# An encoder layer's feed-forward: three of the second half's seven operands are split into high and low parts when they are formed, and the low parts travel through DRAM

## The chip, the cores and the metric

The kernel runs on one core of a Trainium2 chip. The core has a matrix engine (TensorE, PE in the profile; its weight loads stand apart as PEld), a vector engine (VectorE, DVE), a scalar engine (ScalarE, ACT), a general engine (GpSimd, POOL) and an engine that here only issues transfers (SyncE, SP). All transfers that matter go through one queue of SP, which 16 DMA engines serve. Each engine carries out its own instructions in the order in which they were written down for it, and waits where an instruction needs a result of another engine or a landed transfer. The metric is the device time of one execution in microseconds, less being better. The kernel of before took 2279.1 us (median of 3 runs, 2277.12 to 2284.74).

## The reference

The layer works on 2048 tokens of width 1024 in float32. A normalised and modulated input goes through windowed attention and a two-way mLSTM; their outputs are projected and added to the residual stream `x`. The part in question is what follows, a gated feed-forward of width 2816:

```python
hff = rms_norm(x, g_norm2) * (1.0 + scale2) + shift2
gte, up = jnp.split(hff @ w_ffn_in, 2, axis=-1)
ff = (jax.nn.silu(gte) * up) @ w_ffn_out
return x + gate2 * ff
```

A last `rms_norm` follows. The tolerance asks for more than one pass of the fast float32 matmul (the type `fp32r`) gives, so a product of two float32 operands is made of three matmuls: high times high, high times low, low times high. For this every operand exists as a high part (the value rounded to `fp32r` by a copy) and a low part (value minus high part).

## The kernel before

**The products.** The gate and up projections are worked as a two by two block product with seven block products instead of eight. One side are seven weight operands of a 128-column group (`A11`, `A12`, `S2`, `S1`, `S3`, `S4`, `A22`), the other side seven operands made of the normalised tokens, in this order: `B11`, `B21`, `T2`, `T1`, `T3`, `B22`, `T4`. Some of these are sums or differences of others. A token operand has 512 rows of the contraction and 512 token columns, and lies in SBUF as four tiles of 128x1024: two for its high part, two for its low part.

**The units.** `pair` works one unit: the seven products of one column group with one half of the tokens. Each product has four groups of three matmuls (`mm3`, L56 to L58), so a unit has 84 matmuls of 512 columns. There are 22 units for the first half of the tokens (numbered 0 to 21 here) and 22 for the second (22 to 43). Even units belong to the first block column (`half` 0), odd ones to the second up to the turn; odd units leave more sums to POOL and five result tiles to be stored instead of two. Products 0, 2, 4 and 6 add up in one PSUM bank (`ps1`), products 3 and 5 in another (`ps5`), product 1 has a third (`ps2`). Between two products into the same bank ACT has to read the bank out: `s1` after product 0 (L1615), `u2` after product 2 (L1621), `u3` after product 4 (L1629) from `ps1`, and `c5` after product 3 (L1626) from `ps5`. PE can begin product 2, 4, 6 or 5 only when that reading is done; the product in between is the time that ACT has for it. The six tiles that a unit uses for such results (`s1`, `g0`, `t0`, `u2`, `c5`, `u3`) rotate in a pool of six. The results of a unit are stored to `a_d` in DRAM by the next unit's first statement (`stores()`, L1592), and a tile whose store has not landed can't be written again.

**Beside the products.** After product `u` of a unit `beside(u)` runs: it forms the seven weight operands of the next unit (`weights`, a high part by ACT at L1457 and a low part by DVE at L1458 for each, some sums by POOL first), loads the raw weights for the unit after that (`load_raw`), and from unit 2 on, after products 1, 3 and 5, advances by one step a generator (`norm2`) that prepares the second half's token operands: it normalises two blocks of 512 tokens, turns them with PE transposes (`turned`, banks "b" and "d"), forms the seven operands by sums on DVE and stores them unsplit to `hop_d` in DRAM. The first block is copied only; the second block's part walks through four row groups `k`.

**The turn.** Unit 21 is the last of the first half. The token operands of the second half have to come into the same SBUF tiles, so `refill_ops` loads operand `u` after product `u` of unit 21 (`start`, L1414, two transfers of 512 KB into the low part's tiles), and `finish` splits it: ACT copies it into the high part's tiles (L1418), DVE subtracts in place (L1419). `finish` of operands 0 to 3 runs in unit 21 after products 2, 3, 4 and 6, of operands 4 to 6 in unit 22 after products 0, 1 and 3. No weights are formed in unit 21, since units 21 and 22 use the same ones; the raw weights for unit 23 are loaded after product 6 of unit 21.

```python
if turn:
    if u in (2, 3, 4, 6):
        finish_op(min(u - 2, 3))
    if u == 6:
        raw = load_raw(wseq.popleft())
    return
```

The order on each engine is the order of the statements in this part of the program. SP's order is the order of the `dma_start` calls; its queue has eight completion semaphores, which its transfers take in turn (DMAHW0 to DMAHW7 in the listings), so a transfer is issued only when the one eight places ahead of it has landed.

Of the kernel before, what the change touches and what calls it, by code (L numbers as in the profile page):

```python
# [11 lines left out]
F32 = mybir.dt.float32  # L12
F32R = mybir.dt.float32r
BF16 = mybir.dt.bfloat16
I32 = mybir.dt.int32
AF = mybir.ActivationFunctionType
ALU = mybir.AluOpType
MUL, ADD, SUB, MAX, MIN = ALU.mult, ALU.add, ALU.subtract, ALU.max, ALU.min
# [3 lines left out]
P = 128  # L22
# [14 lines left out]
def hybrid_layer_kernel(  # L37
# [5 lines left out]
    pe, dve, act, pool, sp = nc.tensor, nc.vector, nc.scalar, nc.gpsimd, nc.sync  # L43
# [5 lines left out]
    dp = ctx.enter_context(tc.tile_pool(name="dram", bufs=1, space=DRAM))  # L49
    pp = ctx.enter_context(tc.tile_pool(name="psum", bufs=2, space=PSUM))  # L50

    def bank(tag, name):
        return pp.tile([P, 512], F32, tag=tag, name=name, bufs={"g": 2, "a": 2, "b": 1, "c": 2, "d": 1}[tag])
# [16 lines left out]
    bc_d = dp.tile([HM, NT, 4, P], F32, name="bc_d")  # L70
    gate_d = dp.tile([2, D], F32, name="gate_d")
    hop_d = dp.tile([2, 7, 4, P, 512], F32, name="hop_d")
    wo_d = dp.tile([7, 4, P, 512], F32, name="wo_d")
    a_d = dp.tile([7, DFF // P // 2, P, 2, 512], F32, name="a_d")

# [16 lines left out]
    def rsqrt(pl, v, n, d, tag, bufs=2):  # L92

        vv, hh, yi, a = (pl.tile([P, n], dt, tag=tag + i, name=tag + i, bufs=bufs)
                         for i, dt in (("v", F32), ("h", F32), ("y", I32), ("a", F32)))
        y = yi.bitcast(F32)
        o = 0
        for v_, w, d_ in v if isinstance(v, list) else [(v, n, d)]:
            dve.tensor_scalar(vv[:, o:o + w], v_, 1.0 / d_, EPS, MUL, ADD)
            o += w  # L100
        dve.tensor_scalar(yi, vv.bitcast(I32), -0.5, 1597463007.0, MUL, ADD)
        dve.tensor_scalar(hh, vv, -0.5, None, MUL)
        for _ in range(3):
            dve.tensor_tensor(a, y, y, MUL)
            dve.tensor_tensor(a, a, hh, MUL)
            dve.scalar_tensor_tensor(y, a, 1.5, y, ADD, MUL)
        return y
# [40 lines left out]
    def big(i, name, shape=(P, 2, 512), dt=F32R):  # L148

        return hp.tile(list(shape), dt, tag=f"big{i}", name=name)  # L150
# [28 lines left out]
    def turned(t, xt, k, tag, gs, shift):  # L179

        ps = bank(tag, "trn")
        for i in range(4):
            pe.transpose(ps[:, i * P:(i + 1) * P], xt[i][:, k * P:(k + 1) * P], ident)
        act.activation(t, ps, AF.Identity, bias=shift[:, k:k + 1], scale=gs[:, k:k + 1])
# [794 lines left out]
    for i in range(2 * 96 + 60):  # L979
# [3 lines left out]
        if i == 150:  # L983
            t = s2.tile([P, 512], F32, tag="og", name="mqk", bufs=1)
# [300 lines left out]
    class Rows:  # L1285
# [15 lines left out]
        def new(self):  # L1301
            return xd.tile([P, 512], F32, tag="n2", name="n2", bufs=9)
# [58 lines left out]
    def norm2(hh, z, tags, lead):  # L1361
        n = BO[2 * hh + z]
        xt = [pools["ff"].tile([P, D], F32, tag="xt", name="x1t", bufs=4) for _ in range(4)]
        for i in range(4):
            sp.dma_start(xt[i], x1_d[(4 * n + i) * P:(4 * n + i + 1) * P, :])
        op = {o: hop_d[hh, i] for i, o in enumerate(OPS)}
        new = lambda: xp.tile([P, 512], F32, tag="n2", name="n2", bufs=5)
        for _ in range(lead):
            yield True
        ssq = xp.tile([P, 4], F32, tag="ssq", name="ssq")  # L1370
        for i in range(4):
            jk = xp.tile([P, D], BF16, tag="junk", name="junk", bufs=1)
            act.activation(jk, xt[i], AF.Square, accum_out=ssq[:, i:i + 1])
            yield True
        r = rsqrt(xp, ssq, 4, D, "rs")
        yield True
        yield True
        for i in range(4):
            act.activation(xt[i], xt[i], AF.Copy, scale=r[:, i:i + 1])
            yield True  # L1380
        if z == 0:
            for k in range(KT):
                t = new()
                turned(t, xt, k, tags[k % 2], gs2, mod[:, 3, :])
                yield True
                sp.dma_start(op["B11" if k < 4 else "B21"][k % 4], t)
        else:
            for k in range(4):
                b11, b21, b12, b22, t3 = (new() for _ in range(5))
                sp.dma_start(b11, op["B11"][k])  # L1390
                sp.dma_start(b21, op["B21"][k])
                turned(b12, xt, k, tags[0], gs2, mod[:, 3, :])
                yield True
                turned(b22, xt, k + 4, tags[1], gs2, mod[:, 3, :])
                yield True
                dve.tensor_tensor(t3, b22, b12, SUB)
                dve.tensor_tensor(b12, b12, b11, SUB)
                dve.tensor_tensor(b11, b22, b12, SUB)
                yield True
                dve.tensor_tensor(b21, b21, b11, SUB)  # L1400
                for o, t in (("B22", b22), ("T3", t3), ("T1", b12), ("T2", b11)):
                    sp.dma_start(op[o][k], t)
                yield True
                sp.dma_start(op["T4"][k], b21)

    def refill_ops(hh):


        hls = []

        def start(u):
            hls.append([[big(4 * u + 2 * z + i, OPS[u]) for i in range(2)] for z in range(2)])
            for i in range(2):
                sp.dma_start(hls[u][1][i].bitcast(F32), hop_d[hh, u, 2 * i:2 * i + 2].rearrange("k p t -> p k t"))  # L1414

        def finish(u):
            for hi, lo in zip(*hls[u]):
                act.activation(hi, lo.bitcast(F32), AF.Copy)  # L1418
                dve.tensor_tensor(lo, lo.bitcast(F32), hi.bitcast(F32), SUB)  # L1419

        return hls, finish, start
# [10 lines left out]
    def load_raw(j):  # L1432

        v = lambda t: t.rearrange("p (k c) -> p k c", c=P)
        g = wp.tile([P, D], F32, tag="wraw", name="graw", bufs=1)
        a21 = wp.tile([P, 512], F32, tag="oth", name="A21", bufs=1)
        cg, cu = (slice(o + j * P, o + (j + 1) * P) for o in (0, DFF))
        sp.dma_start(v(g), w_ffn_in[:, cg].rearrange("(k p) c -> p k c", p=P))
        sp.dma_start(v(a21), w_ffn_in[0:512, cu].rearrange("(k p) c -> p k c", p=P))
        return (g, a21) if "ff" not in pools and j else (g, a21, load_a22(j))  # L1440
# [45 lines left out]
    for p in range(NPR):  # L1486
# [15 lines left out]
        for i in range(28):  # L1502
# [15 lines left out]
            if p == 0:  # L1518
# [3 lines left out]
                if i in (17, 21):  # L1522
                    hi, lo = (t[i // 21] for t in wo[6])
# [55 lines left out]
    with tc.tile_pool(name="ff", bufs=1, side="right", reuse_waits="tile") as ff:  # L1579
# [84 lines left out]
        pools["ff"] = ff  # L1664
        pools["xp"] = xp
        norms = deque([norm2(1, 0, "bd", 4), norm2(1, 1, "bd", 1)])
        JO = [m * KH + j for j in range(KH) for m in range(2)]
        units = [(0, j) for j in JO] + [(1, j) for j in reversed(JO)]
        wseq = deque(JO[2:] + JO[-2::-1])
        raw, more_w = (*raws[0], load_a22(KH)), None  # L1670
        for n, (hh, j) in enumerate(units[:-1]):
            ws_, turn = nxt_w, n == NJ - 1
            start = lambda u: None
            if turn:
                hop1, finish_op, start = refill_ops(1)
                assert not norms
            STEPS = (0, 0, 1, 1, 2, 2, 1)

            def beside(u):

                nonlocal nxt_w, raw, more_w
                if n in (0, NJ) and u in (0, 1, 3):
                    finish_op(4 + (u + 1) // 2)
                if turn:
                    if u in (2, 3, 4, 6):
                        finish_op(min(u - 2, 3))
                    if u == 6:
                        raw = load_raw(wseq.popleft())
                    return
                if u == 1:  # L1690
                    more_w = weights(raw)
                for _ in range(STEPS[u]):
                    nxt_w = next(more_w)
                if wseq and u == 6 and n != NJ - 2:
                    raw = load_raw(wseq.popleft())
                if n > 1 and u in (1, 3, 5) and norms and next(norms[0], None) is None:
                    norms.popleft()

            pair(hh, j, ws_, hop, start, beside)
            if turn:  # L1700
                hop = hop1
# [263 lines left out]
```

## Time and profile before

| what | value |
|---|---|
| median of 3 runs | 2279.1 us (2277.12 to 2284.74) |
| the profiled execution | 2279.69 us, span 2277.8 us |
| granted TensorE clock over the span | 0.995 |
| PE, DVE, ACT, POOL busy | 98%, 71%, 47%, 47% |
| first half of the feed-forward's products, units 0 to 21 | 994.6 to 1423.1 us of the span |
| second half, units 22 to 43 | 1423.1 to 1848.6 us |
| most units | 19.04 us from start to start |
| unit 22, the first after the turn | 25.65 us |

The times of the trace count from the span's start. A unit's start is the start of its first matmul in the timeline. Units with a PE transpose beside them are 0.5 us longer for each group of four transposes. Since PE is busy almost all the time, time is lost where PE waits, and the waits of other engines matter only where they end in one of PE's.

### The profile page before, as it was taken

How to read it: one execution, taken by the hardware profiler on the slowest of the kernel's cores; microseconds unless marked ns; L12 is line 12 of the kernel's file. 1: busy time of each engine (PE TensorE's matmuls, PEld its weight loads, DVE VectorE, ACT ScalarE, POOL GpSimd, SP SyncE). 2: the span in 40 equal slices, each digit the busy share in tenths (PEclk: the TensorE clock that was granted, in tenths of full speed). 3: DMA queues.
4: the chain of work that ended last, by engine and by line, in shares of the span. 5: the costliest groups of instructions: out<-in, count | busy, mean ns of one | idle time of the engine just before them, and what ended most of it. 6: DMA issues, size and time to landing. Idle time of an engine off the chain costs nothing.

```text
span 2277.8 us, 32434 instructions
## 1 busy us (share of the span) xinstructions
PE 2224.1 (98%) x10822; PEld 1857.4 (82%) x10822; DVE 1613.4 (71%) x2931; ACT 1059.8 (47%) x2206; POOL 1070.8 (47%) x927
## 2 busy tenths in 40 slices
PE   7999999999999989999999999999999999999998
PEld 4997888888888878788888888788888888888886
DVE  6787677656688887786666776766667665785694
ACT  4533656544677756354445444433333333233452
POOL 1006535334344344436666665656566664692020
PEclk8999999999999999999999999999999999999999
DMA  8577755685766576764343454433333374542452
GB/s 318 174 242 224 229 169 166 185 240 172 206 187 180 173 248 203 261 234 151 109 147 111 154 180 158 161 98 111 97 112 97 111 253 145 167 153 93 146 214 93
DMA packets 352811, 391.28 MB, mean 172 GB/s; under 512 B 21260, under 2 KB 251004, under 8 KB 352644
## 3 DMA queue, kind: packets, MB, share of 16 engines
q1 hardware_dynamic: 352420, 389.18, 52.2%
q8 instruction: 85, 1.39, 0.2%
q14 instruction: 82, 0.67, 0.1%
q10 hardware_dynamic: 224, 0.04, 0.0%
HBM read 269.95 MB, written 119.19 MB: 171 GB/s over the span
## 4 chain that ended last, share of the span: by engine, by line
PE 52%; DVE 3%; issue 1%; DMA 1%; ACT 0%; POOL 0%; SPq 0%; DVEq 0%; ACTq 0%; POOLq 0%
PE fp L57 12%; PE fp L56 12%; PE fp L58 12%; PE fo L58 5%; PE fo L57 5%; PE fo L56 5%; DVE al L1719 1%; PE ops L56 1%; DMA al<-a_d 1%; DVE ra L1862 1%; PE ops L58 1%; PE ops L57 1%; DVE w L1728 0%; DVE T L1419 0%; DMA A<-in_w_ffn_in_dram 0%
## 5 line engine op out<-in xcount | busy, mean ns | idle before, releaser
L498 PE MATMUL gps<-hT,whi 128*128 128x512 f32 x1088 | 395.3, 418 | 0.3 <-DVE cacc L513 0.3
L58 PE MATMUL fo<-w,al 128*128 128x512 f32 x616 | 240.0, 390 | 0.8 <-DVE al L1719 0.8
L57 PE MATMUL fo<-w,ah 128*128 128x512 f32 x616 | 239.7, 389 | 0.0
L56 PE MATMUL fo<-w,ah 128*128 128x512 f32 x616 | 239.7, 389 | 0.0
L498 PE MATMUL gps<-hT,wlo 128*128 128x512 f32 x544 | 226.1, 416 | 0.0
L498 PEld LDWEIGHTS gps<-hT,whi 128*128 128x128 f32 x1088 | 199.3, 189 | 24.5 <-DVE cacc L513 0.7
L56 PE MATMUL fp<-T,S 128*128 128x512 f32 x528 | 206.7, 391 | 1.1 <-ACT s L1615 1.1
L57 PE MATMUL fp<-T,S 128*128 128x512 f32 x528 | 205.8, 390 | 0.0
L58 PE MATMUL fp<-T,S 128*128 128x512 f32 x528 | 205.4, 389 | 0.0
L1719 DVE TENSOR_TENSOR al<-al,ah 128x1024 fp32r<-128x1024 f32 x77 | 117.1, 1525 | 108.2 <-ACT ah L1718 108.1
L1718 ACT ACTIVATE ah<-al 128x1024 fp32r<-128x1024 f32 x77 | 81.6, 1059 | 180.9 <-DMA al<-a_d 173.6
L1458 DVE TENSOR_TENSOR S<-sf,S 128x512 fp32r<-128x512 f32 x86 | 130.4, 1554 | 35.9 <-ACT S L1457 35.6
L1458 DVE TENSOR_TENSOR A<-graw,A 128x512 fp32r<-128x512 f32 x86 | 129.6, 1524 | 15.5 <-ACT A L1457 15.5
L1623 DVE SCALAR_TENSOR_TENSOR g<-t,g 128x512 f32<-128x512 f32 x44 | 43.7, 993 | 133.0 <-ACT t L1622 133.0
L58 PE MATMUL fp<-B,A 128*128 128x512 f32 x352 | 136.9, 389 | 0.0
L56 PE MATMUL fp<-B,A 128*128 128x512 f32 x352 | 136.9, 389 | 0.0
L57 PE MATMUL fp<-B,A 128*128 128x512 f32 x352 | 136.9, 389 | 0.0
L58 PEld LDWEIGHTS fo<-w,al 128*128 128x128 f32 x616 | 115.6, 188 | 25.7 <-DVE al L1719 1.7
L56 PEld LDWEIGHTS fo<-w,ah 128*128 128x128 f32 x616 | 115.6, 188 | 24.1
L57 PEld LDWEIGHTS fo<-w,ah 128*128 128x128 f32 x616 | 115.6, 188 | 24.0
L1462 POOL TENSOR_TENSOR sf<-A,A22r 128x512 f32<-128x512 f32 x43 | 60.9, 1417 | 150.2 <-DMA A22r<-in_w_ffn_in_dram 117.6
L798 POOL TENSOR_SCALAR ap<-ap,adn 128x384 f32<-128x384 f32 (+1 forms) x128 | 71.1, 575 | 122.6 <-PE atp L805 66.0
(418 smaller groups left out, 6174.6 us busy)
## 6 DMA issues: line engine op xcount, KB each, us to landing
al<-a_d SPq DMA_DIRECT2D x77, 512.0 KB, 3.7
wmod<-in_w_mod_dram SPq DMA_DIRECT2D x48, 512.0 KB, 7.1
graw<-in_w_ffn_in_dram SPq DMA_DIRECT2D x43, 512.0 KB, 3.6
a_d<-ka SPq DMA_DIRECT2D x66, 256.0 KB, 4.7
bc<-bc_d SPq DMA_DIRECT2D x64, 256.0 KB, 3.7
hop_d<-n SPq DMA_DIRECT2D x56, 256.0 KB, 4.6
a_d<-u SPq DMA_DIRECT2D x55, 256.0 KB, 4.6
mqk<-qk_d SPq DMA_DIRECT2D x44, 256.0 KB, 3.8
```

What stands on the lines that cost most here:

```text
L56: pe.matmul(o, lh, rh, start=first, stop=False, skip_group_check=skip)
L57: pe.matmul(o, lh, rl, start=False, stop=False, skip_group_check=skip)
L58: pe.matmul(o, ll, rh, start=False, stop=last, skip_group_check=skip)
L498: pe.matmul(ps, w[i == 2][:, k, :], hT[n](i == 1, k), start=(k == 0 and i == 0), stop=(k == KT - 1 and i == 2))
L798: pool.tensor_scalar(self.p[g][:, :self.NK], self.p[g][:, :self.NK], dn[:, g:g + 1], 0.0, MUL, ADD)
L1458: dve.tensor_tensor(t[:, 1, :], f, t[:, 0, :].bitcast(F32), SUB)
L1462: pool.tensor_tensor(f1, a21, a22, ADD)
L1623: dve.scalar_tensor_tensor(g0, t0, 1.0, g0, ADD, MUL)
L1718: act.activation(ah, al.bitcast(F32), AF.Copy)
L1719: dve.tensor_tensor(al, al.bitcast(F32), ah.bitcast(F32), SUB)
L1862: dve.tensor_tensor(ra[i], ra[i], xr, ADD)
```

## The change

Operands 4, 5 and 6 of the second half (`T3`, `B22`, `T4`) are split in the generator `norm2`, not at the turn.

- In the generator, each row group `k` of the second block takes five steps instead of four. In the fourth step ACT copies `t3` and `b22` (128x512 each) as rounded high parts into PSUM banks "b" and "d" (`high`). In the fifth step DVE subtracts these from the tiles in place (`low`, one operand in PSUM), the low parts are stored to a new DRAM tensor `hopl_d`, and ACT copies `b21`, which by then holds `T4`, into bank "d". Its subtraction and store are done at the start of the next row group's first step, or after the last one. The unsplit operands are stored to `hop_d` as before; a low part overwrites its tile once that store has landed.
- At the turn, `start` of operands 4 to 6 loads the unsplit operand into the high part's tiles and the low part into the low part's, four transfers of 512 KB instead of two. `finish` of these operands rounds the high part in place on ACT; DVE's six subtractions of 128x1024 are gone.
- The raw weights at the turn are loaded after product 5 of unit 21 instead of after product 6.

```diff
         else:
+            def high(tag, t):
+                h = bank(tag, "hi").bitcast(F32R)
+                act.activation(h, t, AF.Copy)
+                return h
+
+            def low(t, h, o):
+                dve.tensor_tensor(t.bitcast(F32R), t, h.bitcast(F32), SUB)
+                sp.dma_start(o, t)
+
+            left = None
             for k in range(4):
+                if left:
+                    low(*left)
                 b11, b21, b12, b22, t3 = (new() for _ in range(5))
                 sp.dma_start(b11, op["B11"][k])
                 sp.dma_start(b21, op["B21"][k])
...
                 yield True
+                h3, h22 = high(tags[0], t3), high(tags[1], b22)
                 dve.tensor_tensor(b21, b21, b11, SUB)
                 for o, t in (("B22", b22), ("T3", t3), ("T1", b12), ("T2", b11)):
                     sp.dma_start(op[o][k], t)
                 yield True
+                low(t3, h3, hopl_d[0, k])
+                low(b22, h22, hopl_d[1, k])
+                left = b21, high(tags[1], b21), hopl_d[2, k]
                 sp.dma_start(op["T4"][k], b21)
+                yield True
+            low(*left)
...
             for i in range(2):
-                sp.dma_start(hls[u][1][i].bitcast(F32), hop_d[hh, u, 2 * i:2 * i + 2].rearrange("k p t -> p k t"))
+                ks = slice(2 * i, 2 * i + 2)
+                for z, o in ((0, hop_d[hh, u]), (1, hopl_d[u - 4])) if hh and u > 3 else ((1, hop_d[hh, u]),):
+                    sp.dma_start(hls[u][z][i].bitcast(F32), o[ks].rearrange("k p t -> p k t"))
 
         def finish(u):
+            if hh and u > 3:
+                for hi in hls[u][0]:
+                    act.activation(hi, hi.bitcast(F32), AF.Copy)
+                return
...
-                    if u == 6:
+                    if u == 5:
                         raw = load_raw(wseq.popleft())
```

What this does to the order of instructions is shown at three places. In the listings a row has the line, the operation, the tile written and the tiles read, and the semaphores that it waits for. Line numbers after L1385 are those of each kernel: L1414 of before is L1435 of the changed kernel (the turn's loads), L1438 is L1463 (`graw`, raw weights), L1592 is L1617 (stores of results), L1418 is L1443 or, for rounding in place, L1440, and L1457 is L1482.

SP's queue at the turn before, from operand 4 (`T3`) to the first stores of unit 22:

```order
L1414 DMA T3_15404<-hop_d_74 128x2x512 [waits DMAHW1_49,PE_49]
L1414 DMA T3_15405<-hop_d_74 128x2x512 [waits DMAHW2_49,PE_49]
L1414 DMA B22_15428<-hop_d_74 128x2x512 [waits DMAHW3_49,PE_49]
L1414 DMA B22_15429<-hop_d_74 128x2x512 [waits DMAHW4_49,PE_49]
L1414 DMA T4_15449<-hop_d_74 128x2x512 [waits DMAHW5_49,PE_49]
L1414 DMA T4_15450<-hop_d_74 128x2x512 [waits DMAHW6_49,PE_49]
L1438 DMA graw_15459<-in_w_ffn_in_dram 128x8x128 [waits DMAHW7_49,Activation_49]
L1439 DMA A21_15460<-in_w_ffn_in_dram 128x4x128 [waits DMAHW0_49]
L1445 DMA A22r_15463<-in_w_ffn_in_dram 128x4x128 [waits DMAHW1_49]
L1592 DMA a_d_76<-u3_15300 128x512 [waits DMAHW2_49,DVE_49]
L1592 DMA a_d_76<-c5_15299 128x512 [waits DMAHW3_49,Pool_49]
```

and in the changed kernel, from operand 5 (`B22`) on; four transfers for `T3` stand ahead of these:

```order
L1435 DMA B22_15477<-hop_d_74 128x2x512 [waits DMAHW1_49,PE_49]
L1435 DMA B22_15479<-hopl_d_75 128x2x512 [waits DMAHW2_49]
L1435 DMA B22_15478<-hop_d_74 128x2x512 [waits DMAHW3_49,PE_49]
L1435 DMA B22_15480<-hopl_d_75 128x2x512 [waits DMAHW4_49]
L1463 DMA graw_15488<-in_w_ffn_in_dram 128x8x128 [waits DMAHW5_49,Activation_49]
L1464 DMA A21_15489<-in_w_ffn_in_dram 128x4x128 [waits DMAHW6_49]
L1470 DMA A22r_15492<-in_w_ffn_in_dram 128x4x128 [waits DMAHW7_49]
L1435 DMA T4_15506<-hop_d_74 128x2x512 [waits DMAHW0_49,PE_49]
L1435 DMA T4_15508<-hopl_d_75 128x2x512 [waits DMAHW1_49]
L1435 DMA T4_15507<-hop_d_74 128x2x512 [waits DMAHW2_49,PE_49]
L1435 DMA T4_15509<-hopl_d_75 128x2x512 [waits DMAHW3_49]
L1617 DMA a_d_77<-u3_15349 128x512 [waits DMAHW4_49,DVE_49]
```

Six transfers of 512 KB have come in ahead of the stores, and the raw weights have moved ahead of `T4`.

ACT's order in unit 22 before, from the second rounding of `T3` to `u3`:

```order
L1418 ACTIVATE T3_15403<-T3_15405 128x1024 [waits DMAHW2_49]
L1418 ACTIVATE B22_15426<-B22_15428 128x1024 [waits DMAHW3_49]
L1418 ACTIVATE B22_15427<-B22_15429 128x1024 [waits DMAHW4_49]
L1621 ACTIVATE u2_15476<-fp_15479 128x512 [waits DVE_49,PE_49]
L1622 ACTIVATE t0_15475<-g0_15474 128x512 [waits DVE_49,Activation_49]
L1457 ACTIVATE A11_15535<-graw_15459 128x512 [waits DMAHW7_49]
L1626 ACTIVATE c5_15477<-fp_15481 128x512 [waits DMAHW2_49,PE_49,Pool_49]
L1418 ACTIVATE T4_15447<-T4_15449 128x1024 [waits DMAHW5_49]
L1418 ACTIVATE T4_15448<-T4_15450 128x1024 [waits DMAHW6_49]
L1457 ACTIVATE A12_15555<-graw_15459 128x512
L1629 ACTIVATE u3_15478<-fp_15479 128x512 [waits DMAHW3_49,PE_49]
```

and in the changed kernel:

```order
L1440 ACTIVATE T3_15452<-T3_15452 128x1024 [waits DMAHW7_49]
L1440 ACTIVATE B22_15477<-B22_15477 128x1024 [waits DMAHW1_49]
L1440 ACTIVATE B22_15478<-B22_15478 128x1024 [waits DMAHW3_49]
L1646 ACTIVATE u2_15531<-fp_15534 128x512 [waits DVE_49,PE_49]
L1647 ACTIVATE t0_15530<-g0_15529 128x512 [waits DVE_49]
L1482 ACTIVATE A11_15586<-graw_15488 128x512 [waits DMAHW5_49]
L1651 ACTIVATE c5_15532<-fp_15536 128x512 [waits DMAHW4_49,PE_49,Pool_49]
L1440 ACTIVATE T4_15506<-T4_15506 128x1024 [waits DMAHW0_49]
L1440 ACTIVATE T4_15507<-T4_15507 128x1024 [waits DMAHW2_49]
L1482 ACTIVATE A12_15604<-graw_15488 128x512
L1654 ACTIVATE u3_15533<-fp_15534 128x512 [waits DMAHW5_49,PE_49]
```

The order is the same; the in-place roundings wait for other transfers. In both kernels the transfer that `c5` waits for is the store of unit 21's `u3` (DMAHW2 in the one, DMAHW4 in the other), whose tile it takes, and `u3` waits for the store of unit 21's `c5`.

ACT's order at the end of unit 14 before, from the steps after product 5 to `s1` of unit 15; `n2` tiles are the generator's:

```order
L1634 ACTIVATE t0_14193<-u2_14194 128x512 [waits DVE_49,Activation_49]
L1457 ACTIVATE S3_14309<-A21_14178 128x512 [waits DMAHW7_49,Pool_49]
L1457 ACTIVATE S4_14312<-graw_14177 128x512 [waits Pool_49]
L184 ACTIVATE n2_14318<-trn_14323,mod_86,gs2_88 128x512 [waits DMAHW0_49,PE_49]
L1457 ACTIVATE A22_14346<-A22r_14181 128x512
L1615 ACTIVATE s1_14357<-fp_14363 128x512 [waits DMAHW5_49,PE_49]
```

and in the changed kernel, where row group 0 has its fifth step there (`hi` is a PSUM bank):

```order
L1659 ACTIVATE t0_14194<-u2_14195 128x512 [waits DVE_49,Activation_49]
L1482 ACTIVATE S3_14314<-A21_14179 128x512 [waits DMAHW7_49,Pool_49]
L1482 ACTIVATE S4_14317<-graw_14178 128x512 [waits Pool_49]
L1391 ACTIVATE hi_14324<-n2_14101 128x512 [waits DVE_49]
L1482 ACTIVATE A22_14344<-A22r_14182 128x512 [waits DMAHW0_49]
L1640 ACTIVATE s1_14355<-fp_14361 128x512 [waits DMAHW5_49,PE_49]
```

The row `hi` stands between `S4` and `A22`, where the next row group's first turn (L184) stood; that turn has moved to after product 1 of unit 15. `hi` waits until DVE has subtracted bank "d" from `b22`, since the bank is used again.

More of the change, by code (lines that the diff above doesn't have):

```diff
@@ L72, in hybrid_layer_kernel @@
     hop_d = dp.tile([2, 7, 4, P, 512], F32, name="hop_d")
+    hopl_d = dp.tile([3, 4, P, 512], F32, name="hopl_d")
     wo_d = dp.tile([7, 4, P, 512], F32, name="wo_d")
```

## The prediction

> **What bounds the kernel now.** I read the page's busy times first, then PE's waits around the turn, then the timelines of PE, DVE and ACT there, and last the transfers.
>
> ```profile
> PE 2224.1 (98%) x10822; PEld 1857.4 (82%) x10822; DVE 1613.4 (71%) x2931; ACT 1059.8 (47%) x2206; POOL 1070.8 (47%) x927
> ```
>
> PE is the bound, so the change can win only time in which PE waits, and loses only where it makes PE wait. PE's waits from 1400 to 1460 us, and its timeline there (start, duration, line; in brackets the idle time ahead and who ended it):
>
> ```profile
> PE fp L57 <- DVE T L1419: 2.8, 1, 2.8
> PE fp L56 <- ACT c L1626: 0.9, 1, 0.9
> PE fp L57 <- DVE B L1419: 0.3, 1, 0.3
> ...
> 1403.85 0.39 PE L56 MATMUL fp<-B,A 128*128 128x512 f32 x1
> ...
> 1423.10 0.39 PE L56 MATMUL fp<-B,A 128*128 128x512 f32 x1
> ...
> 1437.89 0.50 PE L56 MATMUL fp<-B,S 128*128 128x512 f32 x1 [0.91 <-ACT c L1626]
> ...
> 1440.03 0.50 PE L57 MATMUL fp<-B,S 128*128 128x512 f32 x1 [0.26 <-DVE B L1419]
> ...
> 1444.53 0.50 PE L57 MATMUL fp<-T,A 128*128 128x512 f32 x1 [2.84 <-DVE T L1419]
> ...
> 1446.69 0.63 PE L57 MATMUL fp<-T,A 128*128 128x512 f32 x1
> ...
> 1448.75 0.40 PE L56 MATMUL fp<-B,A 128*128 128x512 f32 x1
> ...
> 1467.80 0.39 PE L56 MATMUL fp<-B,A 128*128 128x512 f32 x1
> ```
>
> The rows that begin a unit are 1403.85, 1423.10, 1448.75 and 1467.80: units 21, 22 and 23 last 19.25, 25.65 and 19.05 us. A product is a seventh of 19.05, 2.72 us. The turn loses 6.6 us in unit 22 and 0.2 in unit 21. That is all there is to gain, 0.3% of the run (also about what a measurement can tell from no change). The queue behind the waits is DVE's:
>
> ```profile
> 1426.79 8.72 DVE L1419 TENSOR_TENSOR T<-T,T 128x1024 fp32r<-128x1024 f32 x4
> 1435.43 0.68 DVE L1618 TENSOR_TENSOR g<-fp,s 128x512 f32<-128x512 f32 x1
> 1436.03 3.95 DVE L1419 TENSOR_TENSOR B<-B,B 128x1024 fp32r<-128x1024 f32 x2
> ...
> 1443.27 2.35 DVE L1419 TENSOR_TENSOR T<-T,T 128x1024 fp32r<-128x1024 f32 x2
> ```
>
> Four subtractions in a row (`T1` and `T3`) make `g` late, so the tanh and `c` late on ACT, which is the 0.9 us wait; `B22` and `T4` end the other two. Transfers and clock in stretches (the last three figures: granted PE clock, DMA share, GB/s):
>
> ```profile
> 1416.00:1422.00 6.00, 6.00 (x28) 4.70 (x27) 5.54 (x5) 5.83 (x7) 1.85 (x1) 1.00 1.05 408
> 1422.00:1428.00 6.00, 6.00 (x28) 4.99 (x27) 5.24 (x6) 3.21 (x6) 1.50 (x2) 1.00 1.05 403
> ...
> 1437.00:1440.00 3.00, 1.88 (x7) 1.24 (x7) 3.00 (x3) 3.00 (x5) 3.00 (x2) 1.00 0.05 19
> 1441.82:1445.23 3.41, 0.70 (x3) 0.61 (x4) 3.41 (x3) 0.00 (x0) 0.97 (x1) 1.00 0.00 0
> 1445.23:1448.65 3.42, 3.42 (x10) 2.64 (x9) 3.42 (x5) 0.00 (x0) 1.60 (x1) 0.50 0.00 0
> ```
>
> Two things decide my forecast. From 1416 on the DMA engines have no gap left, at 403 to 408 GB/s, until the queue is empty at about 1437. And PE's clock was halved for 3.42 us behind a stretch of 3.41 us in which PE worked 0.70: of the 6.6 us lost, 1.6 is that.
>
> **The change: the turn.** Removed are DVE's six subtractions, half of 8.72 plus 3.95 plus 2.35, 10.7 us. DVE is then through with `T1` at 1426.79 + 4.36 = 1431.2 and does `g` at once; no DVE wait is left there.
>
> Added are six transfers of 512 KB, 3.15 MB. At 408 GB/s that is 7.7 us in a queue without a gap, so whatever stands behind `T4` in SP's order lands 7.7 us later. Who waits for these?
>
> ```profile
> 1414.64 1.06 ACT L1418 ACTIVATE B<-B 128x1024 fp32r<-128x1024 f32 x1 [1.31 <-DMA B<-hop_d]
> 1415.91 1.06 ACT L1418 ACTIVATE B<-B 128x1024 fp32r<-128x1024 f32 x1 [0.21 <-DMA B<-hop_d]
> ...
> 1429.72 2.00 ACT L1418 ACTIVATE B<-B 128x1024 fp32r<-128x1024 f32 x2
> 1431.62 0.58 ACT L1621 ACTIVATE u<-fp 128x512 f32<-128x512 f32 x1
> ...
> L1626 ACT ACTIVATE c<-fp 128x512 f32<-128x512 f32 x44 | 26.3, 597 | 35.9 <-PE fp L58 33.1 <-DMA a_d<-u 2.6
> ...
> 1435.17 1.49 POOL L1462 TENSOR_TENSOR sf<-A,A22r 128x512 f32<-128x512 f32 x1 [0.75 <-DMA A22r<-in_w_ffn_in_dram]
> ```
>
> The first two rows give the pace: two transfers of 512 KB land 1.27 us apart. The `L1626` row says that `c` has waited for a store `a_d<-u` before, 2.6 us in all. In unit 22 `c5` takes the tile whose store is the first one behind the turn's loads. Before, that store follows `A22r`, which landed at 1435.17; 256 KB more make it 1435.8, ahead of `c`. Now it lands at 1435.8 + 7.7 = 1443.5.
>
> Step by step in unit 22, in the trace's times. `B22`'s second high part is the 15th load, 14 x 1.27 behind 1414.64 (1432.4) and some tenths more; ACT rounds it (1.0) and reads `u2` (0.6) until about 1434.7, where PE wanted to begin product 4 at 1423.1 + 4 x 2.72 = 1434.0: 0.7 us. Product 4 ends at 1437.4. `c5` starts at 1443.5 and ends at 1444.1; only then may product 5 begin, 6.7 us late. Behind `c5` on ACT wait the roundings of `T4` (landed at about 1442.8; 2.0), `A12` (0.5) and `u3` (0.6): 1447.2, and product 6 needs `u3`. At full clock it would end at 1449.9. But an idle 6.7 us covers a stretch as empty as the one that halved the clock, and by the rows above it comes back after a stretch of full work: with stretches where this trace has them, PE is at half rate from 1444.1 to 1448.65. Half rate costs 0.47 of 4.55 us, 2.1, of which 0.4 is the wait for `u3`. Unit 23 would then start at 1451.6 instead of 1448.75: 2.8 us later. Bounds: 1449.9 (no halving, +1.1) to 1453.0 (+4.2, a stretch begun just before 1444).
>
> The Trainium skill bears on both. "TensorE: Matmul & The Clock Gate", Part 1, says that the gate's window of about 3.4 us runs free of the kernel; 3.41 and 3.42 in these rows agree, and by it the half rate would last 3.4 to 6.8 us here. "DMA: Bandwidth & Descriptors", Where 436 GB/s comes from, lets the memory side bind HBM loads at about 358 GB/s; the trace's 403 to 408 contradict it. By the page the added transfers would take 8.8 us and the sum would be 1.1 us higher (an estimate).
>
> The raw weights, moved ahead of `T4`, land about 2.5 us later than now. POOL starts `sf` then; `A11`'s parts are ready long before unit 23, and the other weights lag as unit 22 does. Rounding in place costs ACT the same 1.0 as now. I take nothing for both.
>
> **The change: the generator.** Twelve high parts (0.6 each by ACT's reads of PSUM; no row writes PSUM from ACT, so 0.5 to 1.1, the 128x1024 copy), twelve low parts, twelve stores of 256 KB.
>
> ```profile
> L1618 DVE TENSOR_TENSOR g<-fp,s 128x512 f32<-128x512 f32 x44 | 30.3, 689 | 32.9 <-issue 32.9
> ...
> 1287.56 0.62 ACT L1457 ACTIVATE S<-graw 128x512 fp32r<-128x512 f32 x1
> ...
> 1288.75 0.62 ACT L1457 ACTIVATE A<-A22r 128x512 fp32r<-128x512 f32 x1
> 1290.03 0.60 ACT L1615 ACTIVATE s<-fp 128x512 f32<-128x512 f32 x1 [0.66 <-PE fp L58]
> ...
> 1287.11 0.39 PE L56 MATMUL fp<-B,A 128*128 128x512 f32 x1
> ...
> 1306.65 0.39 PE L56 MATMUL fp<-B,A 128*128 128x512 f32 x1
> ...
> 1288.38 1.79 DVE L1458 TENSOR_TENSOR S<-graw,S 128x512 fp32r<-128x512 f32 x1
> 1290.09 0.68 DVE L1642 TENSOR_TENSOR ka<-fp,g 128x512 f32<-128x512 f32 x1
> ...
> 1318.09 3.47 DVE L1458 TENSOR_TENSOR A<-graw,A 128x512 fp32r<-128x512 f32 x2
> ...
> 1321.45 0.60 ACT L1629 ACTIVATE u<-fp 128x512 f32<-128x512 f32 x1 [1.38 <-PE fp L58]
> ...
> 1386.60 1.78 DVE L1458 TENSOR_TENSOR S<-graw,S 128x512 fp32r<-128x512 f32 x1
> ...
> 1265.00:1285.00 20.00, 20.00 (x91) 16.54 (x90) 17.11 (x17) 7.97 (x14) 14.58 (x10) 1.00 0.58 198
> ```
>
> A low part is like `L1618`, one operand in PSUM: 0.69 (upper end 1.79, the `S` row with both in SBUF). The stores hide (DMA share 0.58), and so does most of the work, under PE. What does not is the fifth step: ACT's `high` of `b21` waits for DVE's two low parts, and behind it on ACT stands a reading of PSUM that PE needs.
>
> Row group 0 has its fifth step after product 5 of unit 14. DVE ends `S` at 1290.1, the low parts at 1291.4; ACT does `high` to 1292.0, `A22` to 1292.5, `s` to 1293.1. Unit 15 begins 0.5 earlier than now (1287.11), since a group of transposes has left unit 14: at 1286.6. It wants `s` read by 1286.6 + 5.44 = 1292.0: 1.0 us lost. Row group 3 meets the same in units 19 and 20: DVE ends `S` at 1388.4, so `s` ends at 1391.3; unit 20 begins 19.05 ahead of 1403.85, at 1384.8, and wants it by 1390.2: 1.0. Row group 1 has it after product 3 of unit 16: low parts behind 1321.6, `u` read at about 1323.6, while PE wants product 6 at 1306.65 + 16.3 and 0.5 for a group of transposes, 1323.4: 0.2. This lags DVE by some 2 us, and the next low part (end of unit 16) stands behind the same `S`; PE's transposes after product 1 of unit 17 need its bank: about 1.0. Together 3.2 us; 0 if DVE runs 1 us earlier each time, about 12 if a low part takes 1.79.
>
> **The sum.** 2.8 + 3.2 = 6.0 us. The profiled execution took 2279.69 (span 2277.8), so 2285.7; against the median of 2279.1, which is 0.6 below, 2285.1.
>
> **The rivals.** (a) *It does what it removes*: the unit 22 loss goes and the generator hides, 2279.1 - 6.8 = 2272.3. The point that decides is the store behind `T4`: it would have to land by 1436.1, before product 5 wants `c5`, 0.3 us later than now. Against it: 3.15 MB in a full queue. (b) *The turn comes out about even*: no halving of the clock, +1.1, and the generator costs at most 1, so 2280 to 2281. For it: `s` has 0.66 us of idle time ahead of it now, and the stretches may fall well. (c) *The generator costs more*: low parts beside POOL at up to 1.79, each fifth step 2.2 us later, three or four times, and the half rate at its longest: 2289 to 2295. For it: DVE is busy 17.11 of 20 us there.
>
> **How the numbers follow.** Forecast 0.55, own range 2282 to 2289; its spread lies about the line of +0.3% (2285.9), 0.30 below and 0.25 above. (b) 0.18, same. (c) 0.20, slower. (a) 0.07, faster, as its 2272.3 lies just on the line. So faster 0.07, same 0.48, slower 0.45. The range 2278 to 2291 leaves out (a) and the upper part of (c).
>
> **What would show it.** Unit 22 at about 28.5 us; among PE's waits no `L1419` of `T3`, `B22` or `T4`, but ACT `c` with 6 to 7 us, and ACT's `c` idle until DMA `a_d<-u`; the DMA share at 1.0 until about 1445; the clock at 0.5 just behind. In units 14 to 20 waits of PE for `s` (twice, about 1 us) and for a low part ahead of transposes. I am wrong if that store lands early, or if the generator's steps never meet a reading that PE needs.

## The result, and the profile after

| | before | after |
|---|---|---|
| median | 2279.0 us (2276.2 to 2284.7) | 2290.9 us (2288.0 to 2293.7) |
| the profiled execution, span | 2279.7, 2277.8 | 2291.5, 2289.3 |
| units 13 to 20 together | 156.3 us | 163.6 us |
| unit 21 | 19.25 us | 19.42 us |
| unit 22 | 25.65 us | 30.24 us |
| unit 23 | 19.05 us | 19.04 us |

The changed kernel takes 1.0045 times as long, 95% interval 1.0035 to 1.0055: 8 to 12.5 us slower. The units' lengths are differences of the starts of their first matmuls. They hold the whole difference of the two profiled executions (11.8 us): 7.2 us in the generator's units, 0.2 in unit 21 and 4.6 in unit 22, 12.0 in all. PE's work has not grown by that; it waits:

```profile
PE 2227.4 (97%) x10822; PEld 1859.2 (81%) x10822; DVE 1617.8 (71%) x2937; ACT 1065.8 (47%) x2218; POOL 1065.8 (47%) x927
```

**The turn.** First, PE's timeline from unit 21 on; units 21, 22 and 23 begin at 1410.67, 1430.09 and 1460.33. Then SP's and ACT's rows beside it:

```profile
1410.67 0.39 PE L56 MATMUL fp<-B,A 128*128 128x512 f32 x1
...
1430.09 0.39 PE L56 MATMUL fp<-B,A 128*128 128x512 f32 x1
...
1442.22 0.50 PE L56 MATMUL fp<-T,S 128*128 128x512 f32 x1 [1.09 <-ACT u L1646]
...
1452.97 0.80 PE L56 MATMUL fp<-B,S 128*128 128x512 f32 x1 [7.69 <-ACT c L1651]
...
1460.33 0.39 PE L56 MATMUL fp<-B,A 128*128 128x512 f32 x1
```

```profile
1443.47 0.55 SPq L1617 DMA_DIRECT2D a_d<-u  x1
...
1452.32 0.60 ACT L1651 ACTIVATE c<-fp 128x512 f32<-128x512 f32 x1 [8.30 <-DMA a_d<-u]
1452.81 1.99 ACT L1440 ACTIVATE T<-T 128x1024 fp32r<-128x1024 f32 x2
```

The three waits for DVE's subtractions and for `c` behind a late tanh are gone. In their place stands one long wait for `c`, and ACT's row says why: `c5`'s tile still had its store in the queue. SP could issue that store only at 1443.47, 13.4 us after the start of unit 22, and ACT saw it landed at 1452.3, 22.2 us after it. Before, the store left 7.2 us after the start of unit 22 (1423.10) and had landed 12.6 us after it:

```profile
1430.28 1.69 SPq L1592 DMA_DIRECT2D a_d<-u  x1
```

The stretches after (last three figures: PE's granted clock, DMA share, GB/s):

```profile
1436.00:1443.47 7.47, 6.38 (x28) 4.97 (x27) 3.34 (x3) 4.05 (x6) 4.42 (x3) 1.00 1.09 375
1443.47:1450.00 6.53, 1.80 (x8) 1.13 (x6) 0.69 (x1) 0.54 (x1) 3.74 (x3) 1.00 1.02 348
1450.00:1453.39 3.39, 0.42 (x1) 0.42 (x2) 0.00 (x0) 1.07 (x2) 0.00 (x0) 0.50 0.82 315
1453.39:1456.80 3.41, 3.41 (x9) 2.64 (x9) 1.13 (x2) 3.41 (x6) 0.91 (x1) 0.50 0.02 8
```

The transfers have no gap until 1450, but they run at 375 and 348 GB/s there, not at 408. In part that is the raw weights: in the trace their packets of 512 bytes took 27 ns each, those of 2048 bytes 84, and before they brought the rate down too, to 361 GB/s from 1430 to 1434. From 1447 to 1449 no raw weights are left, and the rate is only 245 GB/s; why was not traced. PE's clock is half for two stretches.

**The generator.** PE's four waits in units 15, 16, 18 and 20:

```profile
1292.66 0.50 PE L56 MATMUL fp<-T,S 128*128 128x512 f32 x1 [0.43 <-ACT s L1640]
...
1324.83 0.50 PE L56 MATMUL fp<-T,A 128*128 128x512 f32 x1 [1.01 <-ACT u L1654]
...
1355.53 0.50 PE L56 MATMUL fp<-T,S 128*128 128x512 f32 x1 [2.32 <-ACT s L1640]
...
1396.93 0.50 PE L56 MATMUL fp<-T,S 128*128 128x512 f32 x1 [1.33 <-ACT s L1640]
```

The group of the low parts (min, median, max in ns; then who waited for them, us and times):

```profile
L1395 DVE TENSOR_TENSOR n<-n,hi x12: 671/674/689, 1289.7 to 1398.7; 128x512 fp32r<-128x512 f32 x12
...
  ACT hi L1391: 16.1, 4
  PE trn L184: 0.4, 2
```

ACT stood still four times, 16.1 us together, for the bank that `b21`'s high part takes from `b22`'s. Three of PE's waits are the readings behind that. The fourth and largest, in unit 18, I had not foreseen; it starts at SP, more than a unit earlier. Rows of SP, ACT, POOL and DVE after, then of SP and DVE before:

```profile
1333.38 0.32 SPq L1396 DMA_DIRECT2D hopl_d<-n  x1
...
1334.73 1.68 SPq L1463 DMA_DIRECT2D graw<-in_w_ffn_in_dram  x1
...
1340.20 0.63 ACT L1482 ACTIVATE A<-graw 128x512 fp32r<-128x512 f32 x1 [2.17 <-DMA graw<-in_w_ffn_in_dram]
...
1341.95 1.76 POOL L1487 TENSOR_TENSOR sf<-A,A22r 128x512 f32<-128x512 f32 x1 [6.24 <-ACT A L1482]
...
1342.48 1.78 DVE L1409 TENSOR_TENSOR n<-n,n 128x512 f32<-128x512 f32 x1
...
1347.59 3.48 DVE L1483 TENSOR_TENSOR S<-sf,S 128x512 fp32r<-128x512 f32 x2
```

```profile
1330.06 0.38 SPq L1438 DMA_DIRECT2D graw<-in_w_ffn_in_dram  x1
...
1330.66 0.69 DVE L1397 TENSOR_TENSOR n<-n,n 128x512 f32<-128x512 f32 x1
```

The raw weights left SP 3.4 us after the start of unit 17 before (1326.69) and 7.1 us after it now (1327.68), behind a store that waits for VectorE's low part. So POOL forms its sums when DVE forms the generator's, and beside POOL DVE's subtraction with both operands in SBUF takes 1.78 us instead of 0.69. (The Trainium skill, "SBUF — State Buffer", Who interferes with whom, says that such an instruction contends with GpSimd's reads and that one with at most one operand in SBUF does not; the low parts' 671 to 689 ns agree.) All of it ends as a late `s` in unit 18.

### The profile page after: what moved, and what is told of

Its sections match the earlier page's. It is cut to its first block, busy times and chain, and to the rows that moved or that the text cites. A ratio compares the mean times of both kernels' runs of the same rounds, so it can differ in the third digit from the quotient of the medians.

```text
span 2289.3 us, 32466 instructions
## 1 busy us (share of the span) xinstructions
PE 2227.4 (97%) x10822; PEld 1859.2 (81%) x10822; DVE 1617.8 (71%) x2937; ACT 1065.8 (47%) x2218; POOL 1065.8 (47%) x927
## 4 chain that ended last, share of the span: by engine, by line
PE 52%; DVE 3%; DMA 1%; issue 1%; ACT 1%; POOL 0%; SPq 0%; ACTq 0%; DVEq 0%; POOLq 0%
PE fp L56 11%; PE fp L57 11%; PE fp L58 11%; PE fo L56 6%; PE fo L57 6%; PE fo L58 6%; DVE S L1483 1%; PE ops L56 1%; PE ops L58 1%; PE ops L57 1%; DMA a_d<-u 0%; PE trn L184 0%; DMA graw<-in_w_ffn_in_dram 0%; DMA T<-hop_d 0%; DMA B<-hop_d 0%
```

## Experiments

Ratios are against the kernel before on the same chip, with 95% intervals. "Lost" in units 13 to 20 is against their 156.3 us before.

| kernel | ratio | units 13 to 20, lost | unit 21 | unit 22 |
|---|---|---|---|---|
| after | 1.0045 (1.0035 to 1.0055) | 7.2 | 19.42 | 30.24 |
| generator alone | 1.0033 (1.0023 to 1.0043) | 7.4 | 20.05 | 25.62 |
| turn alone | 1.0019 (1.0010 to 1.0028) | 0.0 | 19.04 | 30.18 |
| free tiles | 1.0040 (1.0027 to 1.0052) | 7.4 | 20.28 | 27.33 |
| free tiles, raw weights behind `T4` | 1.0037 (1.0024 to 1.0049) | 7.2 | 19.95 | 27.92 |
| store a step later | 1.0037 (1.0025 to 1.0050) | 5.7 | 20.85 | 30.27 |
| bank c | 1.0040 (1.0028 to 1.0053) | 8.4 | 20.78 | 30.72 |
| both generator edits | 1.0021 (1.0011 to 1.0031) | 0.5 | 20.50 | 31.36 |
| `T3` and `T4` | 1.0004 (0.9995 to 1.0013) | 3.2 | 19.04 | 25.35 |
| `T4` | 0.9982 (0.9973 to 0.9991) | 0.0 | 19.15 | 23.26 |
| `T4`, free tiles | 0.9973 (0.9963 to 0.9983) | 0.0 | 19.77 | 20.56 |

**Each half alone.** The generator alone, with the turn of before (the changed kernel's lines are the removed ones):

```diff
-                for z, o in ((0, hop_d[hh, u]), (1, hopl_d[u - 4])) if hh and u > 3 else ((1, hop_d[hh, u]),):
-                    sp.dma_start(hls[u][z][i].bitcast(F32), o[ks].rearrange("k p t -> p k t"))
+                sp.dma_start(hls[u][1][i].bitcast(F32), hop_d[hh, u, 2 * i:2 * i + 2].rearrange("k p t -> p k t"))
...
-            if hh and u > 3:
-                for hi in hls[u][0]:
-                    act.activation(hi, hi.bitcast(F32), AF.Copy)
-                return
...
-                    if u == 5:
+                    if u == 6:
```

> The generator as in the changed kernel (three operands split when formed, low parts stored), the turn as before (tiles loaded whole, split by ScalarE and VectorE, raw weights loaded with product 6's step); the stored low parts are not read. Theory 1, the two halves of the change add: units 13 to 20 lose what they lost in the changed kernel, 7.2 us against before (unit 18 alone 4.3), the turn nothing, so unit 22 lasts 25.6 us and the time is 2279.0 + 7 = 2286 us. Rival, part of the loss in units 15 to 20 comes from something else of the change (other places of tiles, the turn's own loads): units 13 to 20 lose under 4 us and the time is below 2283. Rival, the generator's stores and waits also reach into the turn: unit 22 is over 27 us and the time over 2287.5.

The turn alone, with the generator of before:

```diff
-                for z, o in ((0, hop_d[hh, u]), (1, hopl_d[u - 4])) if hh and u > 3 else ((1, hop_d[hh, u]),):
+                for z, o in ((0, hop_d[hh, u]), (1, hop_d[hh, u])) if hh and u > 3 else ((1, hop_d[hh, u]),):
...
-                low(t3, h3, hopl_d[0, k])
-                low(b22, h22, hopl_d[1, k])
-                left = b21, high(tags[1], b21), hopl_d[2, k]
```

> The turn as in the changed kernel, the generator as before. The low parts of the three operands are not formed: their tiles are loaded a second time from the whole operand, so the bytes and instructions of the turn are those of the changed kernel but the split of these three operands is left out of what is computed. Theory 1, the two halves add: units 13 to 20 last as before (0 +- 0.6 us), units 21 and 22 together lose 4.8 us, unit 22 lasts 30.2 us, and the time is 2279.0 + 4.8 = 2284 us. Rival, the turn was late only because the generator left queues or rows behind it: units 21 and 22 lose under 2 us and the time is at most 2281.

PE's waits from unit 15 to 22 of the generator alone, and then of the turn alone (us, times, longest):

```profile
PE fp L56 <- ACT s L1634: 3.2, 3, 2.0
PE fp L57 <- DVE T L1438: 2.9, 1, 2.9
PE fp L56 <- ACT c L1645: 1.6, 2, 0.9
PE fp L56 <- ACT u L1648: 1.0, 1, 1.0
```

```profile
PE fp L56 <- ACT c L1632: 7.6, 1, 7.6
PE fp L56 <- ACT u L1627: 0.2, 1, 0.2
```

The halves add. Alone they cost 0.33% and 0.19%, together 0.52%, against the 0.45% of the change. Neither reaches into the other's stage, but for 0.8 us in unit 21 of the generator alone (the last section returns to it), so the rivals fall; the turn lost 4.3 us where I had expected 4.8, and most of the difference lies in unit 21.

**The turn: who is waited for.** `c5` and `u3` of unit 22 from a pool that is idle there:

```diff
             s1_, g0, t0, u2, c5, u3 = (ot(n) for n in ("s1", "g0", "t0", "u2", "c5", "u3"))
+            if (hh, j) == (1, JO[-1]):
+                c5, u3 = (xp.tile([P, 512], F32, tag="n2", name=n, bufs=5) for n in ("c5", "u3"))
```

> The changed kernel, with the two tiles that unit 22 takes for c5 and u3 from a pool that is idle there, so that they no longer stand for the stores of an earlier unit that lie behind the turn's loads in SyncE's queue. Theory 1, unit 22's 30.2 us are set by c5's wait for that store (7.7 us on TensorE): the wait goes, the next thing that is late is T4's own tiles (landed 21.5 us after the unit's start) with ScalarE's rounding behind them, unit 22 lasts 24.5 to 26 us and the time is 2290.9 - 5 = 2286 us. Rival, the landing of the loads sets the unit's end and c5's wait only stands beside it: unit 22 stays above 29 us and the time within 1 us of 2290.9.

```profile
1455.00 1.06 ACT L1440 ACTIVATE T<-T 128x1024 fp32r<-128x1024 f32 x1 [3.17 <-DMA T<-hop_d]
...
1457.11 0.50 PE L56 MATMUL fp<-T,A 128*128 128x512 f32 x1 [4.68 <-ACT u L1656]
```

The wait for the store is gone, and 2.9 us of unit 22 with it, not 4 to 6: `T4`'s tiles, landed 20.8 us after the unit's start, hold ACT and `u3` behind it. That `T4` comes next was right; that it would cost so much, and still halve the clock, was not. In the time the gain can't be told from none.

So `T4` was loaded ahead of the raw weights again:

```diff
-                    if u == 5:
+                    if u == 6:
```

> The changed kernel with c5 and u3 of unit 22 in free tiles, and the raw weights loaded behind T4's tiles as before the change. Theory 1, after c5's wait is gone T4's landing sets unit 22 (27.3 us with it at 20.8 us after the start): T4's last tile lands 2.5 to 3.5 us earlier, unit 22 lasts 23 to 25 us and the time is about 2 to 3 us below that of the free tiles alone, 2287 us. Rival, the end is set by the raw weights' own splitting, which then comes later: unit 22 stays above 26.5 us.

```profile
1450.23 0.63 ACT L1482 ACTIVATE A<-graw 128x512 fp32r<-128x512 f32 x1 [5.92 <-DMA graw<-in_w_ffn_in_dram]
1450.77 0.58 ACT L1653 ACTIVATE c<-fp 128x512 f32<-128x512 f32 x1
...
1451.40 0.79 PE L56 MATMUL fp<-B,S 128*128 128x512 f32 x1 [4.53 <-ACT c L1653]
```

A miss: the rival held. `T4` is on time and the raw weights are late, 18.8 us after the unit's start (1431.39). ACT rounds the first of them ahead of `c`, so the same `c` is late by another way. With 3 MB more, in both orders that were run what stands last in the queue comes too late for something in unit 22; the order only chose what.

**The generator: what holds `s` and `u`.** The store of `b21`'s low part a step later, behind the raw weights' load (`sub_low` is `low` without its store):

```diff
             for k in range(4):
+                late_low = left
                 if left:
-                    low(*left)
+                    sub_low(*left[:2])
...
                 yield True
+                if late_low:
+                    sp.dma_start(late_low[2], late_low[0])
                 turned(b22, xt, k + 4, tags[1], gs2, mod[:, 3, :])
```

> The changed kernel, with the store of the low part of b21 issued one step later, behind the next raw-weight load in SyncE's queue. Theory 1, unit 18's loss of 3.3 us beyond a transpose group's 0.5 comes from that load, which stood 4.7 us behind a store that waited for VectorE: the load is issued near 1330 us as before, unit 18 lasts 19.0 to 20.5 us, units 13 to 20 together lose 3.5 to 4.5 us instead of 7.2, and the time is 2290.9 - 3 = 2288 us. Rival, unit 18 is late because ScalarE rounds two more tiles ahead of s and VectorE's subtractions take 1.7 us beside GpSimd: unit 18 stays above 22.5 us and the time within 1 us of 2290.9.

Its high part in a bank with two buffers:

```diff
-                left = b21, high(tags[1], b21), hopl_d[2, k]
+                left = b21, high("c", b21), hopl_d[2, k]
```

> The changed kernel, with the high part of b21 in PSUM bank c (two buffers) instead of bank d, so that ScalarE need not wait there until VectorE has formed b22's low part. Theory 1, the losses of units 15, 16 and 20 (0.7, 1.25 and 1.6 us) and a part of unit 18's are this wait on ScalarE with s or u behind it: these units fall to 19.0 to 20.0 us, units 13 to 20 lose 2 to 4 us instead of 7.2 and the time is 2290.9 - 4 = 2287 us. Rival, VectorE's backlog delays s and u by other ways (the tanh step that they stand behind): units 15, 16 and 20 stay within 0.3 us of the changed kernel, and so does the time within 1 us.

> Both edits on the generator together: the store of b21's low part one step later (which took unit 18 from 23.4 to 21.3 us by itself) and b21's high part in bank c. Theory 1, what was left in unit 18 is s and u behind the same wait on ScalarE: unit 18 lasts 19.0 to 20.0 us, units 13 to 20 lose at most 1.5 us against before, and the time is 2290.9 - 6 = 2285 us, before plus the turn's 4 to 5 us. Rival, VectorE's own added work in the generator is what counts: units 13 to 20 lose 4 us or more and the time stays above 2287.

Each edit alone missed its forecast: with the later store units 13 to 20 still lose 5.7 us (expected 3.5 to 4.5), with bank c 8.4 (expected 2 to 4), and neither ratio can be told from the change's 1.0045. The later store takes unit 18 from 23.4 to 21.3 us; in bank c units 15 and 16 fall to 20.0 and 19.9 us, as expected, unit 20 only to 20.4, and unit 18 rises to 26.2. SP's and PE's rows of bank c:

```profile
1336.00 0.42 SPq L1463 DMA_DIRECT2D graw<-in_w_ffn_in_dram  x1
...
1357.32 0.79 PE L56 MATMUL fp<-T,S 128*128 128x512 f32 x1 [2.96 <-ACT s L1640]
```

The raw weights leave 7.4 us after the start of unit 17 (1328.61) there, `s` is late by 2.96, and the 0.79 us of the matmul behind it is the half clock. With both edits they leave 3.2 us after it (1327.06):

```profile
1330.26 0.38 SPq L1469 DMA_DIRECT2D graw<-in_w_ffn_in_dram  x1
```

and unit 18 lasts 20.04 us; from unit 13 to the end of unit 20 the list of waits holds none of PE's, and the generator's loss is 0.5 us. So both causes are shown: the wait for a bank on ACT, and the raw weights behind a store on SP. VectorE's added work, the rival, costs at most that 0.5 us. The kernel stays slower because the turn is untouched; its waits in units 21 and 22:

```profile
PE fp L56 <- ACT c L1657: 9.2, 2, 8.1
PE fp L56 <- ACT u L1652: 1.4, 1, 1.4
```

**The size.** If the added bytes decide at the turn, fewer operands must do better. On the kernel before: `T4` alone formed split, its high part in bank c a step after the sum, its low part and the store in the next step; raw weights last, and the free tiles:

```diff
             for k in range(4):
-                b11, b21, b12, b22, t3 = (new() for _ in range(5))
+                b11, b12, b22, t3 = (new() for _ in range(4))
                 sp.dma_start(b11, op["B11"][k])
-                sp.dma_start(b21, op["B21"][k])
+                if k:
+                    sp.dma_start(op["T4"][k - 1], b21)
+                    left = b21, high(b21), hopl_d[0, k - 1]
                 turned(b12, xt, k, tags[0], gs2, mod[:, 3, :])
                 yield True
+                if left:
+                    low(*left)
                 turned(b22, xt, k + 4, tags[1], gs2, mod[:, 3, :])
                 yield True
+                b21 = new()
+                sp.dma_start(b21, op["B21"][k])
...
+                for z, o in ((0, hop_d[hh, u]), (1, hopl_d[0])) if hh and u == 6 else ((1, hop_d[hh, u]),):
```

> From the kernel before: T4 alone of the three operands is formed split (its high part in bank c, its store away from the raw weights), its low part adds 1 MB to the turn's loads instead of 3; raw weights behind T4 as before; c5 and u3 of unit 22 in free tiles. Theory 1, the gain that was meant exists where the added loads stay in the shadow of the products: T4's two subtractions leave the turn, on which TensorE waited 2.84 us, no half clock, unit 22 lasts 19.5 to 21.5 us instead of 25.65, units 13 to 20 lose 0 to 2 us, the time is 2279.0 - 4 = 2275 us. Rival, any split in the generator costs its 7 us and any added load ends the turn later: unit 22 stays above 24 us and the time above 2280.

PE's waits in units 21 to 23, and no half clock:

```profile
PE fp L56 <- ACT c L1654: 1.3, 2, 0.9
PE fp L56 <- ACT s L1643: 1.1, 1, 1.1
```

Unit 22 lasts 20.56 us, the generator's units what they did, and the kernel is faster than before by 0.27% (0.17 to 0.37). Unit 23 gives 1.4 us back, the `s` above. Units 21 to 23 together are 3.2 us shorter than in the profile of before, while the medians differ by 6.1 us; where the rest comes from is not shown. The free tiles alone were not run on the kernel before, but its trace leaves them nothing to win there: `c5`'s store had landed 12.6 us after the start of unit 22, and ACT came to `c` at 14.2. Without the free tiles:

> T4 alone formed split, as in the faster kernel, but c5 and u3 of unit 22 in the tiles that they had before, which stand for stores behind the turn's loads. Theory 1: with 1 MB more to load that store lands near 14.7 us after unit 22's start and c would be copied at 14.2, so c5's wait costs about 0.6 us: unit 22 lasts 20.6 to 22 us and the time is 2276 to 2278 us. Rival, the wait is long enough to bring the half clock: unit 22 is over 23 us and the time over 2279.

```profile
1439.14 0.60 ACT L1652 ACTIVATE c<-fp 128x512 f32<-128x512 f32 x1 [1.17 <-DMA a_d<-u]
...
1439.79 0.77 PE L56 MATMUL fp<-B,S 128*128 128x512 f32 x1 [2.19 <-ACT c L1652]
```

`c` waits for the store again, 1.17 us instead of the 0.6 expected, and that brings the half clock, as the rival said: 23.26 us. The time, 2277.5 us, is theory 1's all the same, and the intervals of the two kernels' ratios overlap. With `T3` split too, its high part also in bank c:

> T3 and T4 formed split, B22 not; free tiles for c5 and u3 of unit 22; raw weights behind T4. The turn's loads grow by 2 MB. Theory 1, the added megabytes decide: with 1 MB the raw weights land 12.5 us after the start of unit 22 and it lasts 20.6 us, with 3 MB 18.8 us and 27.9 us; with 2 MB they land near 15.5 us, ScalarE copies c behind their rounding at 16 us, TensorE waits 2 to 3 us at product 5, unit 22 lasts 21.5 to 24 us and the time is 2277 to 2280 us. Rival, VectorE's subtractions decide, of which two more are gone: g is formed on time, unit 22 lasts 19.0 to 20.5 us and the time is at most 2275.

```profile
PE fp L56 <- DVE n L1395: 2.6, 2, 1.8
```

```profile
1445.29 0.63 ACT L1486 ACTIVATE A<-graw 128x512 fp32r<-128x512 f32 x1 [4.59 <-DMA graw<-in_w_ffn_in_dram]
...
1446.46 0.79 PE L56 MATMUL fp<-B,S 128*128 128x512 f32 x1 [3.17 <-ACT c L1657]
```

The added megabytes decide. The raw weights are rounded 15.8 us after the unit's start (1429.49); they were rounded at 13.7 with one added megabyte, where ACT waited not for them but for `g`, and at 18.8 with three, and unit 22 lasts 25.35, 20.56 and 27.92 us. VectorE's shorter work, the rival, does not help: the tanh step of `g` runs 10.6 us after the unit's start instead of 13.1 with `T4` alone, and the unit is longer all the same. My sizes missed: unit 22 lies 1.4 us above my range, with the clock halved for 6.83 us, which I had left out, and the generator loses 3.2 us that I had put at nothing, as `T3`'s high part stays in bank c until the next step, and PE waits there for its low part, 2.6 us.

## Why the prediction was right, and where its sizes were off

The sign was right and, but for unit 18, the mechanism: slower, because the turn's gain is spent in the queue of transfers and the fifth step of the generator meets readings that PE needs. The size was half of what came, +6.0 us against some 10 to 12. The measured time lies in the predicted range but above the forecast's own (2282 to 2289), where rival (c) stood; yet (c)'s reason for the low parts (1.79 us each) is not what happened; only its half rate at the longest is. So it is in part luck that the range held: its upper end was there for slow low parts, and what filled it was unit 18 (3.3 us) and a turn 2.0 us longer than forecast.

- *Six subtractions leave, no DVE wait is left at the turn*: right; the waits of 2.84 and 0.26 us are gone.
- *The store behind `T4` lands 7.7 us later*: 9.6 us later. The bytes were right, the rate was not: 375 and 348 GB/s from 1436 to 1450, not the 408 of the stretch that I took it from. The raw weights' part of that fall was in the queue before as well; the fall to 245 GB/s behind them is new, and its cause stays open. This is the turn's mis-sized term.
- *`c` waits 6.7 us, `u2` 0.7*: 7.69 and 1.09.
- *Half clock for 4.55 us*: 6.83 us, of which PE was idle for the first 3.0 and lost 0.47 of the other 3.8 us, 1.8; predicted 2.1. (In the turn alone it lasted 10.24 us.) Together the turn lost 4.8 us, predicted 2.8 and at most 4.2.
- *Raw weights ahead of `T4`, taken at nothing*: not settled. The turn with `T4` first and the free tiles is no shorter (27.92 against 27.33 us), but that compares two different waits.
- *Low parts 0.69 us, high parts 0.6*: right, 0.674 and 0.594 at the median.
- *Fifth step, units 15, 16, 17 and 20: 1.0, 0.2, 1.0, 1.0*: beyond the transposes' 0.5 us for each group units 15, 16, 17 and 20 lost 0.7, 1.2, 0.4 and 1.6 us: 3.9 in all, predicted 3.2.
- *The stores hide*: this step failed. By DMA share they do, but in SP's order the store of `b21`'s low part stands ahead of the next raw weights and waits for VectorE. Unit 18 lost 3.3 us for it and for the bank, and the two edits together took all of it back. I had counted the queue's bytes and not its head.

## What to carry to other kernels

A precomputed part that is fetched again must fit where the transfers have room: here one of three operands pays, two come out even and three cost. At each wait that an instruction brings into an in-order queue (a store that waits for VectorE on SP, a reading of a bank on ACT) look at what stands behind it, a unit further on too. Where two causes lie in series, an edit to one of them shows little, so try both together before either is dropped.

## What the runs showed of the hardware

Shorter waits than I had counted on were followed by the half clock. PE in stretches of about 3.41 us, laid out from a change of the granted clock in the same trace, with free tiles and the raw weights behind `T4`, and then with the free tiles alone:

```profile
1354.02:1357.43 3.41, 1.50 (x7) 1.24 (x7) 3.41 (x3) 1.88 (x4) 3.25 (x3) 1.00 0.06 17
1357.43:1360.84 3.41, 3.41 (x9) 2.63 (x8) 3.41 (x6) 0.00 (x0) 2.83 (x2) 0.50 1.08 329
```

```profile
1355.11:1358.53 3.42, 1.48 (x7) 0.90 (x5) 3.03 (x4) 3.42 (x7) 2.12 (x2) 1.00 0.00 0
1358.53:1361.94 3.41, 3.34 (x15) 2.75 (x16) 3.41 (x4) 0.02 (x1) 3.25 (x3) 1.00 0.64 184
```

A wait of 1.9 us was enough in the first (PE busy 1.50 of 3.41 us, then half rate), while a wait of 2.0 us in the second (1.48) was not. So PE need not be idle for a whole stretch, and near 1.5 us of work in one either can follow; a wait's length alone does not tell. Its place counts too: in the changed kernel the wait of 2.32 us that ends at 1355.53 lay across the border of two such stretches, at 1354.4 (PE busy 2.22 and 2.29 of 3.41 us), and the clock stayed full.

Unit 21 varied between 19.04 and 20.85 us over kernels whose turn is the same up to there. The traces show what sets it: ACT's first rounding of `B11` begins 10.0 to 12.4 us after the unit's start, `c` stands behind both roundings of `B11`, and from about 10.6 us on unit 21 grows by as much as that rounding is late, as PE waits for `c` at product 5. The loads left SP 5.4 to 6.9 us after the unit's start, behind the stores of unit 20's results, which explains a part; why they also landed later was not traced. It is up to 1.8 us of spread in each comparison of two profiles.
